# Stacking the high and low parts of the queries in the score products of a dilated-attention kernel

## The chip, the cores and the metric

The kernel runs on one core of one Trainium2 chip. The metric is the device time of one execution in microseconds (us). The engines of the core go by these names: PE is TensorE (matmuls; PEld is its weight loads), DVE is VectorE, ACT is ScalarE, POOL is GpSimd, and SP issues most of the DMAs.

## What is computed

Two layers over 1024 positions of width 1024, batch 1, all in float32. Layer 0 mixes tokens with a chunked gating MLP, layer 1 with dilated sliding-window attention. A dense MLP with squared ReLU follows each mixer. The diff touches the attention of layer 1 alone, of which this is the core (cut from the reference):

```python
WINDOW_DILATIONS = ((128, 1), (512, 4), (2048, 16))     # 3 groups, 8 heads of 64 in each
def _dilated_group(q, k, v, bias_table, window, dilation):
    ...
    s = jnp.einsum('bnqrhc,bnkrhc->bnrhqk', qb, kc) * (HEAD_DIM ** -0.5)
    ...
    logits = jnp.where(valid[None, :, None, None], s + bias[None, None, None], NEG_INF)
    m = jnp.max(logits, axis=-1)
    p = jnp.exp(logits - m[..., None])
    den = jnp.sum(p, axis=-1)
    num = jnp.einsum('bnrhqk,bnkrhc->bnqrhc', p, vc)
    ...
```

The three groups are merged for each head by their denominators, and a projection follows.

## The kernel before

**Precision.** Products run in the float32r format. A float32 operand is split into a high part (a rounding copy on ACT) and a low part (source minus high part, on DVE). A product is then the sum of three: high by high, high by low, low by high.

**Units of attention.** Two heads of 64 channels lie together on the 128 partitions. There are 4 such head pairs and 3 dilation groups, so 12 units, taken for each pair in the order group 1, group 2, group 0 (dilations 4, 16, 1). `unit_qk` computes q and k of a unit (128 channels by 1024 positions) with seven block products instead of eight, in a Strassen-like scheme, each of 12 matmuls of 512 columns. Their results come up one half of the positions at a time, and `halves` (lines 1432 to 1437) makes the high and low parts of such a half: one ACT activation and one DVE operation over 128 partitions by 512 columns. It is called four times in a unit: q first half, k second half, q second half, k first half. The results go to four tiles of 128 by 1024, in an order of positions that puts the positions of one residue side by side. So for the dilations 4 and 16 the write has a stride (`permuted`, line 1216), and for dilation 1 it is contiguous.

**Scores.** `scores` (line 1491) is called four times in a unit (48 times in all), each time for two blocks of 128 queries and two heads. Each block and head takes three products of 64 rows (the channels of one head); head 0 lies on rows 0 to 63, head 1 on rows 64 to 127, and the products of the two heads alternate. The moving operand has 128 or 256 columns of keys. That is 12 products in a call. Behind it, DVE adds the bias and takes the extreme (line 1511), ACT takes the exponential (line 1513), PE transposes the probabilities (line 204), ACT and DVE split them (lines 225 and 226), and PE multiplies by the values; ACT and DVE then take that result out (lines 1551 and 1552).

**Order.** The order of PE's instructions is the order in which the program writes them. A small planner (`Flow`) advances a clock with each matmul (columns times 0.422 ns) and slips the steps of scores, transposes and value products between the block products when their due time on that clock has come; the scores of a unit are due 4200 ns of that clock after its q and k were issued. `flow.until` holds the second k half of a unit back until the scores of the unit before were issued. The order on the other engines is the scheduler's; operations marked `high_priority` are taken as if they stood 60 instructions earlier.

**Memory.** A pool `tpool` holds 13 temporaries of 128 by 512 under the tag "t" and 4 landing buffers under the tag "r" (`raw`, line 178), into which weights are loaded. PSUM's eight banks are three for block products ("mm") and five for the rest ("at").

Of the kernel before, what the change touches and what calls it, by code (L numbers as in the profile page):

```python
# [12 lines left out]
F32 = mybir.dt.float32  # L13
F32R = mybir.dt.float32r
AF = mybir.ActivationFunctionType
ALU = mybir.AluOpType
# [3 lines left out]
P = 128  # L20
D = 1024
S = 1024
HALF = 512
# [12 lines left out]
def blk(b, n=1):  # L36
    return slice(b * P, (b + n) * P)
# [91 lines left out]
def trunk(ctx: ExitStack, tc: tile.TileContext, xT, w_u, w_v, w_o, w_s, b_s, w_qkv, w_vt, w_bo, rel,  # L129
          w_up, w_dn, w_dl, vecs, onehot, outT):  # L130
    nc = tc.nc
# [5 lines left out]
    tpool = ctx.enter_context(tc.tile_pool(name="tpool", bufs=13))  # L137
# [2 lines left out]
    psa = ctx.enter_context(tc.tile_pool(name="psa", bufs=8 - MMB, space=PSUM))  # L140
    dram = ctx.enter_context(tc.tile_pool(name="dram", bufs=2, space=DRAM))
    ctx.enter_context(tc.manual_schedule(engines={mybir.EngineType.PE}))

    def temp():
        return tpool.tile([P, HALF], F32, tag="t", name="t")
# [7 lines left out]
    def slot(shape=(P, S), dtype=F32, name="s"):  # L153

        return slots.tile(list(shape), dtype, tag="s", name=name)
# [20 lines left out]
        return Pair(wpool.tile([P, 2, HALF], F32R, tag="w", name=name))  # L176

    def raw():
        return tpool.tile([P, HALF], F32, tag="r", name="r", bufs=4)

    def load(src, t=None):

# [7 lines left out]
    def mm_bank():  # L190
        return psm.tile([P, HALF], F32, tag="mm", name="mm")
# [4 lines left out]
    def matmul(out, lhsT, rhs, passes=1, **kw):  # L196
        nc.tensor.matmul(out, lhsT, rhs, **kw)  # L197
        n = 1
        for d in rhs.shape[1:]:
            n *= d  # L200
        flow.pe(max(n, 64) * COL * passes)
# [154 lines left out]
    def product(bank, w, xs, more=False):  # L356

        for k, x in enumerate(xs):
            three(bank, w, blk(k), x, not more and k == 0, k == len(xs) - 1, skip_group_check=True)
            flow.pump()  # L360
# [373 lines left out]
    for gi, chunks in enumerate(((0, 1, 2), (3, 4, 5), (6, 7))):  # L734
        banks = {}
        for k in range(KT):
# [35 lines left out]
            for e, i, n, f in order:  # L772
                x, c = ys[n // 4][k], blk(n % 4)
                matmul(banks[n, f], x[e == 1][:, c], w[e == 2][:, half(f)], start=(k == 0 and e == 0),
                       stop=(k == 7 and e == 2))
# [29 lines left out]
    for tiles in ((0, 1, 2), (3,), (4,), (5, 6, 7)):  # L805
# [3 lines left out]
        for s in range(2):  # L809
            for i, m in enumerate(tiles):  # L810
                b = mm_bank()
# [9 lines left out]
    for tiles in ((0, 1), (2,), (3,), (4, 5, 6, 7)):  # L821
        w = [weight(w_o[m]) for m in tiles]
        for s in range(2):
            for i, m in enumerate(tiles):
                b = mm_bank()
# [356 lines left out]
    hd = [[dram.tile([P, HALF], F32, name=f"hd{m}_{s}", bufs=1) for s in range(2)] for m in range(KT)]  # L1182
# [10 lines left out]
    def bias_tile(hp, g):  # L1193

        off = bvec.offset + (2 * hp * 3 + g) * VEC
        rev = temp()
        w = 2 * P if g < 2 else P
        if g < 2:
            nc.sync.dma_start(rev.rearrange("p (a b) -> p a b", a=2),
                              bass.AP(tensor=bvec.tensor, offset=off, ap=[[1, P], [3 * VEC, 2], [1, 2 * P]]))  # L1200
        else:
            nc.vector.memset(rev[:, 0:2 * P], NEG)
            for r in range(2):
                nc.sync.dma_start(
                    rev[64 * r:64 * r + 64, 0:2 * P].rearrange("p (a b) -> p a b", a=2)[:, :, 64 - 64 * r:128 - 64 * r],
                    bass.AP(tensor=bvec.tensor, offset=off + 64, ap=[[1, 64], [3 * VEC, 2], [1, 64]]))
        return rev, w

    def bias_turn(rev, w):
        t = spare().rearrange("p (a b) -> p a b", a=2)  # L1210
        src = rev[:, 0:2 * w]
        nc.vector.tensor_copy(t[:, :, 0:w], bass.AP(tensor=src.tensor, offset=src.offset + w - 1,
                                                    ap=[list(src.ap[0]), [w, 2], [-1, w]]))
        return t

    def permuted(t, s, g):

        d = DIL[g]
        if g == 0:
            return t[:, half(s)]  # L1220
        n = HALF // d
        return t.rearrange("p (r q) -> p q r", r=d)[:, s * n:(s + 1) * n, :]

    def own(t, g):
        return t if g == 0 else t.rearrange("p (q r) -> p q r", r=DIL[g])
# [8 lines left out]
    for hp, g in units:  # L1234
        u = Unit()
# [154 lines left out]
    def v_load(i):  # L1390

        u = U[i]
        if 0 < i < NU - 1:
            yield U[i - 1].pv, 0
        u.V = [slot((P, 4, 4, 64), F32R, "V") for _ in range(2)]
        src = vd[i // 4][:, i % 4]
        for e in range(2):
            t = u.V[e].bitcast(F32).rearrange("p b a c -> p b (a c)")
            if u.g == 0:
                parts = [(t, src.rearrange("(e b p) a c -> e p b (a c)", e=2, p=P)[e])]  # L1400
            elif u.g == 1:
                parts = [(t, src.rearrange("(e p b) a c -> e p b (a c)", e=2, p=P)[e])]
            else:
                x = src.rearrange("(q e b r) a c -> e r q b (a c)", q=64, e=2, b=4)
                parts = [(t[64 * r:64 * r + 64], x[e, r]) for r in range(2)]
            for dst, part in parts:
                vloads[i] = nc.sync.dma_start(dst, part).ins
        yield LAT["vd"]
        u.v.t = flow.t
# [5 lines left out]
    def unit_qk(i):  # L1415

        u = U[i]
        g, w = u.g, unit_w[i]
        if i == 0:
            u.bias = bias_turn(*u.rev)  # L1420
        if i < NU - 1:
            flow.add(v_load(i))
            U[i + 1].rev = bias_tile(U[i + 1].hp, U[i + 1].g)
        x = terms_a.t
        qk = {}

        def place_of(m, s):
            if m not in qk:
                qk[m] = [slot((P, S), F32R, f"{'qk'[m]}{e}") for e in range(2)]
            return [permuted(t, s, g) for t in qk[m]]  # L1430

        def halves(m, s, src):
            hi, lo = place_of(m, s)
            sc = -0.125 if m == 0 else 1.0
            with tc.high_priority(offset=PRIO):
                nc.scalar.activation(hi, src, AF.Copy, scale=sc)
                nc.vector.scalar_tensor_tensor(lo, src, sc, hi.bitcast(F32), op0=ALU.mult, op1=ALU.subtract)

        def total(x0, x1, t=None):
            t = temp() if t is None else t  # L1440
            with tc.high_priority(offset=PRIO):
                nc.vector.tensor_tensor(t, x0, x1, op=ALU.add)
            return t

        def copied(out, src):
            with tc.high_priority(offset=PRIO):
                nc.scalar.activation(out, src, AF.Copy)
            return out

        a = mm_bank()  # L1450
        product(a, w[1], x[1])
        more()
        sums = copied(mm_bank(), a)
        d = mm_bank()
        product(d, w[5], x[5])
        more()
        k1 = copied(temp(), d)
        product(sums, w[6], x[6], True)
        more()
        q1 = copied(temp(), sums)  # L1460
        product(a, w[2], x[2], True)
        more()
        halves(0, 0, own(a, g))
        product(sums, w[7], x[7], True)
        more()
        if i > 0:
            flow.until(lambda: U[i - 1].scored.t is not None)
        if i < NU - 1:
            U[i + 1].bias = bias_turn(*U[i + 1].rev)
        halves(1, 1, own(total(k1, sums, k1), g))  # L1470
        product(d, w[3], x[3], True)
        more()
        halves(0, 1, own(total(q1, d, q1), g))
        product(sums, w[4], x[4], True)
        more()
        halves(1, 0, own(sums, g))
        u.q, u.k = qk[0], qk[1]
        u.qk.t = flow.t

# [11 lines left out]
    def scores(u, j):  # L1491
        keys, at, width = geometry(u.g, j)
        sb = [at_bank(), at_bank()]
        for i in range(2):
            kc = blk(*keys[i])
            c = slice(at[i], at[i] + keys[i][1] * P)
            for a, b in ((0, 0), (0, 1), (1, 0)):
                for hd in range(2):
                    r = slice(64 * hd, 64 * hd + 64)
                    matmul(sb[hd][:, c], u.q[a][r, blk(2 * j + i)], u.k[b][r, kc],  # L1500
                           start=(a == 0 and b == 0), stop=(a == 1))
        ps = []
        for hd in range(2):
            p = temp()
            for i in range(2):
                w = keys[i][1] * P
                c = slice(at[i], at[i] + w)
                m, dn = u.st[:, 2 * j + i, hd, 0:1], u.st[:, 2 * j + i, hd, 1:2]
                bt = u.bias[:, hd, 0:P] if u.g == 2 else u.bias[:, hd, 2 * P - w:2 * P]
                with tc.high_priority(offset=PRIO):  # L1510
                    nc.vector.tensor_tensor_reduce(out=p[:, c], in0=sb[hd][:, c], in1=bt, op0=ALU.add, op1=ALU.min,
                                                   scale=1.0, scalar=BIG, accum_out=m)
                    nc.scalar.activation(p[:, c], p[:, c], AF.Exp, bias=m, scale=-1.0, accum_out=dn)
            ps.append(p)
        return ps
# [297 lines left out]
    for i in range(NU):  # L1813
        unit_qk(i)
# [136 lines left out]
```

## Time and profile before

| | |
|---|---|
| median of 3 runs | 2115.53 us (2114.2 to 2117.39) |
| the profiled execution, its own time | 2117.96 us |
| its span, first to last instruction | 2116.2 us, mean granted TensorE clock 0.998 |
| busy over the span | PE 99%, PEld 82%, DVE 75%, ACT 56%, POOL 23% |
| score products | 576, from 1073.2 to 1428.5 us of the span |

Times in the profile count from the span's start. A group of instructions has its line in the kernel, its engine, the output and input tiles by name, the shape, a count, the busy time in us and the mean of one in ns, and behind the bar the idle time just ahead of them with what ended it. L197 and L204 are the lines of the helpers for all matmuls and all transposes. Matmuls overlap in the pipeline, so the pace of PE is read from the starts and not from the durations.

### The profile page before, as it was taken

The numbers are of one execution on the slowest core, as the hardware profiler recorded it, in microseconds if no ns is written. First come the engines' busy times: TensorE is split into PE (matmuls) and PEld (weight loads), VectorE is DVE, ScalarE is ACT, GpSimd is POOL, SyncE is SP. The second block draws the span as 40 slices with busy tenths as digits, with TensorE's granted clock in tenths as the row PEclk, the third lists the DMA queues.
The fourth block names the chain that finished last, engine by engine and source line by source line (L and its number), as shares of the span: only waits on it lengthen the run. The fifth ranks groups of instructions, "written<-read, shape, count | busy, mean of one in ns | idle before, by whom it ended". The sixth has DMA issues, their size and how long they took to land.

```text
span 2116.2 us, 30735 instructions
## 1 busy us (share of the span) xinstructions
PE 2093.6 (99%) x10160; PEld 1731.2 (82%) x10160; DVE 1577.5 (75%) x2902; ACT 1182.7 (56%) x2387; POOL 495.5 (23%) x368
## 2 busy tenths in 40 slices
PE   9999999999999999999999999999999999999998
PEld 7888888888888888788888888888888888888887
DVE  7878769766689999787746666757985456988876
ACT  7645436566675555345456665776556556544432
POOL 2000124323224333430000000002442222433244
PEclk9999999999999999999999999999999999999999
DMA  6428814588766666644865657582266443655432
GB/s 220 130 94 294 305 34 139 196 281 278 258 208 204 231 209 225 222 162 164 308 194 160 176 156 185 157 270 79 71 205 198 156 154 127 203 164 161 143 115 80
DMA packets 224757, 387.10 MB, mean 183 GB/s; under 512 B 39898, under 2 KB 67669, under 8 KB 224597
## 3 DMA queue, kind: packets, MB, share of 16 engines
q1 hardware_dynamic: 215456, 383.77, 55.1%
q10 hardware_dynamic: 9140, 1.36, 0.4%
q8 instruction: 80, 1.31, 0.3%
q14 instruction: 81, 0.66, 0.1%
HBM read 252.24 MB, written 132.81 MB: 182 GB/s over the span
## 4 chain that ended last, share of the span: by engine, by line
PE 88%; DVE 6%; DMA 3%; issue 1%; ACT 1%; POOL 0%; SPq 0%; DVEq 0%; POOLq 0%; ACTq 0%
PE mm L197 45%; PE at L197 41%; PE at L204 2%; DVE y L226 1%; DMA t<-in_w_qkv 1%; DVE t L226 1%; DMA r<-in_w_v 1%; DMA h<-in_xT 0%; DVE r L443 0%; DVE hx L226 0%; DVE tr L226 0%; DVE wp L226 0%; DMA t<-hid_(1, 0)_6229 0%; DMA r<-in_w_vt 0%; DVE b L448 0%
## 5 line engine op out<-in xcount | busy, mean ns | idle before, releaser
L226 DVE TENSOR_TENSOR wp<-r,wp 128x512 fp32r<-128x512 f32 (+3 forms) x399 | 328.2, 828 | 121.8 <-ACT wp L225 119.2
L225 ACT ACTIVATE wp<-r 128x512 fp32r<-128x512 f32 (+3 forms) x399 | 236.0, 596 | 316.7 <-PE at L197 194.5
L197 PE MATMUL mm<-t,wp 128*128 128x512 f32 x1368 | 345.2, 396 | 0.2 <-DVE t L1001 0.2
L197 PE MATMUL at<-hx,wp 128*128 128x512 f32 x1452 | 341.1, 389 | 1.7 <-DVE h L1079 1.5
L197 PEld LDWEIGHTS at<-hx,wp 128*128 128x128 f32 x1452 | 272.2, 188 | 60.0 <-DVE h L1079 3.2
L197 PEld LDWEIGHTS mm<-t,wp 128*128 128x128 f32 x1368 | 250.7, 188 | 53.0 <-issue 0.7
L283 POOL TENSOR_TENSOR t<-t 128x512 f32<-128x512 f32 (+1 forms) x60 | 76.2, 1271 | 810.3 <-ACT t L278 808.1
L197 PE MATMUL at<-y,wp 128*128 128x512 f32 x1008 | 245.3, 389 | 0.0
L197 PE MATMUL mm<-hx,wp 128*128 128x512 f32 x984 | 234.3, 389 | 0.1
L197 PEld LDWEIGHTS at<-y,wp 128*128 128x128 f32 x1008 | 189.1, 188 | 39.5 <-issue 0.4
L197 PEld LDWEIGHTS mm<-hx,wp 128*128 128x128 f32 x984 | 184.6, 188 | 38.9 <-ACT mm L1102 0.5
L197 PE MATMUL mm<-y,wp 128*128 128x512 f32 x816 | 210.3, 397 | 1.2 <-DVE y L226 0.6
L381 POOL TENSOR_TENSOR t<-r 128x512 f32<-128x512 f32 (+3 forms) x62 | 82.5, 1331 | 477.7 <-DMA r<-in_w_up 121.3
L197 PEld LDWEIGHTS mm<-y,wp 128*128 128x128 f32 x816 | 149.1, 188 | 33.4 <-DVE y L226 1.1
L226 DVE TENSOR_TENSOR hx<-t,hx 128x512 fp32r<-128x512 f32 x192 | 161.5, 845 | 6.5 <-ACT hx L225 6.3
L197 PE MATMUL mm<-y,whi 128*128 128x512 f32 x512 | 158.4, 390 | 1.2 <-DVE t L789 1.2
L197 PE MATMUL at<-t,wp 128*128 128x512 f32 x552 | 130.6, 389 | 0.0
L225 ACT ACTIVATE hx<-t 128x512 fp32r<-128x512 f32 x192 | 118.7, 627 | 20.8 <-DMA t<-hid 12.5
L383 POOL TENSOR_TENSOR r<-r 128x512 f32<-128x512 f32 (+3 forms) x62 | 91.0, 1468 | 167.2 <-DVE wp L226 146.9
L197 PEld LDWEIGHTS at<-t,wp 128*128 128x128 f32 x552 | 103.6, 188 | 21.5
L1079 DVE TENSOR_TENSOR h<-h,at 128x512 f32<-128x512 f32 x144 | 97.6, 678 | 25.6 <-PE at L197 25.1
L197 PEld LDWEIGHTS mm<-y,whi 128*128 128x128 f32 x512 | 95.5, 188 | 21.0 <-issue 1.6
(247 smaller groups left out, 3481.3 us busy)
## 6 DMA issues: line engine op xcount, KB each, us to landing
t<-hid SPq DMA_DIRECT2D x182, 256.0 KB, 4.2
wd<-tr SPq DMA_DIRECT2D x154, 256.0 KB, 3.1
wp<-wd SPq DMA_DIRECT2D x77, 512.0 KB, 4.2
hid<-t SPq DMA_DIRECT2D x140, 256.0 KB, 2.9
r<-in_w_up SPq DMA_DIRECT2D x120, 256.0 KB, 2.9
r<-in_w_dn SPq DMA_DIRECT2D x80, 256.0 KB, 2.6
hid<-b SPq DMA_DIRECT2D x56, 256.0 KB, 2.9
r<-in_w_v SPq DMA_DIRECT2D x48, 256.0 KB, 3.1
```

What stands on the lines that cost most here:

```text
L197: nc.tensor.matmul(out, lhsT, rhs, **kw)
L204: nc.tensor.transpose(out, src, ident)
L225: return (nc.scalar.activation(hi, src, AF.Copy).ins, (engine or nc.vector).tensor_tensor(lo, src, hi.bitcast(F32), op=ALU.subtract).ins)
L226: (engine or nc.vector).tensor_tensor(lo, src, hi.bitcast(F32), op=ALU.subtract).ins)
L283: nc.gpsimd.tensor_tensor(self.acc, self.acc, sq, op=ALU.add)
L381: tt(r3, r[0, 0], r[1, 0], op=ALU.subtract)
L383: tt(r[1, 1], r[1, 0], r[0, 0], op=ALU.subtract)
L1079: return engine.tensor_tensor(hs[i, s], hs[i, s], src, op=ALU.add).ins
```

## The change

The query tiles and the key tiles are laid out anew, by head. For head 0 the query tile has the high part on rows 0 to 63 and the low part on rows 64 to 127; for head 1 it is the other way round. The key tile of a head has the high part of that head's keys on both halves of the rows. A third tile has the low parts of the keys of both heads. One product over 128 rows of a head's query tile and key tile then gives high by high and low by high at once, and one product over 64 rows with the third tile gives high by low. A call of `scores` has 4 products of 128 rows and then 4 of 64 rows.

`halves` is cut by head: two ACT activations and two DVE operations over 64 partitions each, and for k two more ACT copies, which are not marked `high_priority`, to fill the other half of the rows. The source of the last `halves` of a unit is first copied from PSUM to a temporary by ACT. The third tile has two buffers of 128 by 1024, for which room is made by closing the pool of the four landing buffers `raw`; the helper `roomy` opens one of the two pools at a time in the same place.

```diff
+    def roomy(name, bufs):
+        if name not in held:
+            room.close()
+            held.clear()
+            held[name] = room.enter_context(tc.tile_pool(name=f"{name}{len(opened)}", bufs=bufs))
+            opened.append(name)
+        return held[name]
...
     def raw():
-        return tpool.tile([P, HALF], F32, tag="r", name="r", bufs=4)
+        return roomy("raws", 4).tile([P, HALF], F32, tag="r", name="r")
+
+    def lows():
+        return roomy("lows", 2).tile([P, S], F32R, tag="kl", name="kl")
...
-                qk[m] = [slot((P, S), F32R, f"{'qk'[m]}{e}") for e in range(2)]
+                qk[m] = [slot((P, S), F32R, f"{'qk'[m]}{e}") for e in range(2)] + [lows()] * m
             return [permuted(t, s, g) for t in qk[m]]
 
         def halves(m, s, src):
-            hi, lo = place_of(m, s)
+            to = place_of(m, s)
             sc = -0.125 if m == 0 else 1.0
+            rows = [slice(0, 64), slice(64, 128)]
             with tc.high_priority(offset=PRIO):
-                nc.scalar.activation(hi, src, AF.Copy, scale=sc)
-                nc.vector.scalar_tensor_tensor(lo, src, sc, hi.bitcast(F32), op0=ALU.mult, op1=ALU.subtract)
+                for hd, r in enumerate(rows):
+                    nc.scalar.activation(to[hd][r], src[r], AF.Copy, scale=sc)
+                for hd, r in enumerate(rows):
+                    lo = to[2][r] if m else to[hd][rows[1 - hd]]
+                    nc.vector.scalar_tensor_tensor(lo, src[r], sc, to[hd][r].bitcast(F32), op0=ALU.mult,
+                                                   op1=ALU.subtract)
+            if m:
+                for hd, r in enumerate(rows):
+                    nc.scalar.activation(to[hd][rows[1 - hd]], to[hd][r].bitcast(F32), AF.Copy)
...
-        halves(1, 0, own(sums, g))
+        halves(1, 0, own(copied(temp(), sums), g))
...
-            for a, b in ((0, 0), (0, 1), (1, 0)):
-                for hd in range(2):
-                    r = slice(64 * hd, 64 * hd + 64)
-                    matmul(sb[hd][:, c], u.q[a][r, blk(2 * j + i)], u.k[b][r, kc],
-                           start=(a == 0 and b == 0), stop=(a == 1))
+            for hd in range(2):
+                matmul(sb[hd][:, c], u.q[hd][:, blk(2 * j + i)], u.k[hd][:, kc], start=(i == 0), stop=False,
+                       skip_group_check=True)
+        for i in range(2):
+            kc = blk(*keys[i])
+            c = slice(at[i], at[i] + keys[i][1] * P)
+            for hd in range(2):
+                r = slice(64 * hd, 64 * hd + 64)
+                matmul(sb[hd][:, c], u.q[hd][r, blk(2 * j + i)], u.k[2][r, kc], start=False, stop=(i == 1),
+                       skip_group_check=True)
```

More of the change, by code (lines that the diff above doesn't have):

```diff
@@ L142, in trunk @@
     ctx.enter_context(tc.manual_schedule(engines={mybir.EngineType.PE}))
+    room = ExitStack()
+    ctx.enter_context(room)
+    held = {}
+    def roomy(name, bufs):
[5 more added lines that the diff above has]
+        return held[name]
+    opened = []
     def temp():
```

## The prediction

> **What bounds the kernel now.** I read the page first, then the busy time by stretch over the attention stage, then the timeline around a few score blocks.
>
> ```profile
> span 2116.2 us, 30735 instructions
> PE 2093.6 (99%) x10160; PEld 1731.2 (82%) x10160; DVE 1577.5 (75%) x2902; ACT 1182.7 (56%) x2387; POOL 495.5 (23%) x368
> ...
> PE 88%; DVE 6%; DMA 3%; issue 1%; ACT 1%; POOL 0%; SPq 0%; DVEq 0%; POOLq 0%; ACTq 0%
> ```
>
> PE is busy 99% of the span and carries 88% of the chain that ended last. So the time falls only where PE gets less to do, and rises by every stall that the change puts into PE's order. The diff acts in the twelve attention units, about 1058 to 1418 us, plus four score blocks just after.
>
> ```profile
> core 0: us, PE busy (x) PEld busy (x) DVE busy (x) ACT busy (x) POOL busy (x), PEclk, DMA share, GB/s
> 1058.00:1418.00 360.00, 358.06 (x2242) 295.15 (x2241) 228.53 (x737) 231.12 (x652) 0.00 (x0) 1.00 0.62 186
> ```
>
> PE has 2 us of idle in 360; ACT works 64% and DVE 63% of the stage, at full clock. That looks like room for more work on ACT and DVE, but it is a mean, and below I look at the stretches where the new work would lie.
>
> **What the score products cost today.** 576 products of 64 rows, twelve to a block, 48 blocks. The next fence holds the two groups, then weight loads seen through two slits of 10 to 15 ns, then PE around two score blocks and one value block.
>
> ```profile
> L197 PE MATMUL at<-k,q 64*128 64x128 f32 x312 | 26.2, 285 | 1.9 <-DVE t L1688 1.9
> L197 PE MATMUL at<-k,q 64*128 64x256 f32 x264 | 23.3, 294 | 0.0
> 1073.33 0.19 PEld L197 LDWEIGHTS at<-k,q 64*128 64x128 f32 x2
> 1073.44 0.19 PEld L197 LDWEIGHTS at<-k,q 64*128 64x128 f32 x2
> 1073.23 0.96 PE L197 MATMUL at<-k,q 64*128 64x128 f32 x12
> 1074.12 0.97 PE L197 MATMUL mm<-t,wp 128*128 128x512 f32 x3
> ...
> 1085.37 1.03 PE L197 MATMUL at<-tr,V 128*128 128x256 f32 x8
> 1086.24 0.90 PE L197 MATMUL mm<-t,wp 128*128 128x512 f32 x3
> 1086.98 0.82 PE L204 MATMUL at<-ident,t 128*128 128x128 f32 x6
> 1087.73 0.95 PE L197 MATMUL at<-k,q 64*128 64x128 f32 x12
> ```
>
> The weight loads of the two heads (rows 0 to 63 and 64 to 127) run together: both slits show two loads of 0.19 us begun in the same hundredth, the next two 0.11 later. So twelve products are six slots of two. A block takes 1074.12 - 1073.23 = 0.89 us: six slots of 0.11 = 0.66, and 0.23 for starting and for going back to 128 rows. The value block, eight products of 128 rows, takes 1086.24 - 1085.37 = 0.87, or 0.109 each, and those go one by one.
>
> **PE's part of the change.** Removed: six double slots, 0.66. Added: four products of 128 rows, 4 x 0.109 = 0.44, and two double slots, 0.22. Together 0.66 again. A product over 128 rows costs as much as two over 64 that run side by side, so stacking high and low saves a product, not a slot. The 0.23 stays, because there is still one passage from 128 to 64 rows and one back. I take 0. Six transposes take 1087.73 - 1086.98 = 0.75 before a score block instead of 6 x 0.109 = 0.65, so a passage is worth about 0.10: if it hides better, or costs once more, that is 0.10 x 48 = 5 us down or up. [...]
>
> **ACT and DVE, the operations.** Times in ns are least, median and greatest of twelve; the least is a unit of dilation 1 (written contiguously, 4 units), the median one of dilation 4 or 16 (written with a stride, 8 units).
>
> ```profile
> L1436 ACT ACTIVATE q<-mm x12: 570/1082/1093, 1060.5 to 1397.7; 128x512 fp32r<-128x512 f32 x12
> L1436 ACT ACTIVATE q<-t x12: 631/1124/1135, 1066.8 to 1407.4; 128x512 fp32r<-128x512 f32 x12
> L1437 DVE SCALAR_TENSOR_TENSOR q<-t,q x12: 691/1096/1205, 1067.9 to 1408.0; 128x512 fp32r<-128x512 f32 x12
> L1447 ACT ACTIVATE t<-mm 128x512 f32<-128x512 f32 x24 | 14.1, 587 | 5.5 <-PE mm L197 5.1
> L1551 ACT ACTIVATE N<-at 64x256 f32<-64x256 f32 x96 | 36.4, 379 | 35.0 <-DVE N L1552 20.1 <-PE at L197 11.1 <-PE at L204 2.1
> L225 ACT ACTIVATE tr<-at 128x256 fp32r<-128x256 f32 x32 | 10.5, 377 | 8.6 <-PE at L204 8.5
> L1552 DVE TENSOR_TENSOR N<-N,at 64x256 f32<-64x256 f32 x96 | 40.1, 417 | 52.8 <-ACT N L1551 52.0
> L226 DVE TENSOR_TENSOR tr<-at,tr 128x256 fp32r<-128x256 f32 x32 | 12.2, 419 | 9.8 <-ACT tr L225 9.6
> ```
>
> An activation over 64 partitions takes what one over 128 takes (379 against 377 ns for 256 elements), and so on DVE (417 against 419). So each of the four `halves` of a unit, now cut by head, costs twice its ACT and twice its DVE time; each of the two for k adds two ACT copies; and one ACT copy of PSUM to a temporary (0.59) comes in. The moves between partition halves are nothing new: line 1551 does them.
>
> In a strided unit ACT gains one activation for each q half (1.08 + 1.12), three for each k half (6 x about 1.1) and 0.59: 9.4 us. Neighbours overlap by about 0.1 us in the timeline, which leaves about 8.6. In a contiguous unit it is 8 x 0.6 + 0.59 = 5.4, with overlap 5.0. DVE gains four operations: 4 x 1.1 = 4.4 or 4 x 0.69 = 2.8. Over twelve units that is 8 x 8.6 + 4 x 5.0 = 89 us on ACT, 231 + 89 = 320 of 360: no bound yet by the mean.
>
> The copies read and write with a stride; no ACT row has both. DVE's low part reads the strided high part and writes with a stride, at 1.10 against 0.69 contiguous, no worse than ACT's strided write alone (1.12 against 0.63). So I take 1.1; if reading cost a second 0.49, it would be 32 copies x 0.49 = 16 us of ACT more, and a gain is excluded, since a copy is not shorter than the contiguous 0.6. [...]
>
> **Where they lie.** Scores of a unit begin when its q and k are there, and PE's order is fixed. I take for each kind of unit the stretch from its first write of q to its first score product: there all the added work must be done. The last four rows below show how that is read for the fifth unit (group 2).
>
> ```profile
> 1060.40:1073.20 12.80, 12.80 (x57) 10.33 (x56) 5.63 (x6) 6.30 (x6) 0.00 (x0) 1.00 0.73 250
> 1083.50:1102.30 18.80, 18.80 (x113) 15.72 (x111) 13.68 (x35) 12.49 (x33) 0.00 (x0) 1.00 0.69 178
> 1142.40:1162.60 20.20, 20.18 (x130) 16.89 (x126) 17.47 (x60) 15.64 (x38) 0.00 (x0) 1.00 0.46 145
> 1177.40:1196.50 19.10, 18.46 (x113) 15.26 (x112) 15.88 (x33) 13.22 (x28) 0.00 (x0) 1.00 0.53 167
> 1209.00:1225.50 16.50, 16.50 (x99) 13.68 (x97) 9.03 (x26) 8.10 (x24) 0.00 (x0) 1.00 0.61 169
> 1177.44 1.08 ACT L1436 ACTIVATE q<-mm 128x512 fp32r<-128x512 f32 x1 [0.37 <-DVE t L1688]
> ...
> 1192.17 1.07 ACT L1436 ACTIVATE k<-mm 128x512 fp32r<-128x512 f32 x1
> ...
> 1193.63 1.14 DVE L1437 SCALAR_TENSOR_TENSOR k<-mm,k 128x512 fp32r<-128x512 f32 x1
> ...
> 1196.46 0.89 PE L197 MATMUL at<-k,q 64*128 64x128 f32 x12
> ```
>
> ACT's busy time is the fourth figure with a count. First unit: 6.3 + 8.6 - 12.8 = 2.1 us too much. Second: 12.5 + 8.6 - 18.8 = 2.3. Fourth (group 1, later parts; the seventh and tenth are built alike): 15.6 + 8.6 - 20.2 = 4.0, three times. Fifth (with the eighth and eleventh): 13.2 + 8.6 - 19.1 = 2.7, three times. The contiguous units: 8.1 + 5.0 is under 16.5, nothing. Sum: 2.1 + 2.3 + 12.0 + 8.1 = 24.5 us by which PE stands before a unit's first scores. DVE in the fourth: 17.5 + 4.4 = 21.9 in 20.2, over by less than ACT, so it is not added.
>
> The chain of one unit says the same. In the fifth, k is ready at 1193.63 + 1.14 = 1194.77, 1.69 us ahead of the scores. Behind the last product there would now be a copy (0.59), two activations (2.2) and two copies (2.2) instead of 1.07 + 1.14 on ACT and DVE: 5.0 against 2.2 is 2.8 longer, 1.1 over the slack, with the doubled q part queued ahead of it. In ACT's queue the next unit's copies, exponentials and value evacuations stand behind these, and PE's transposes and value products wait on those.
>
> Two corrections, one each way: splits for value products that are due only after the scores can wait (about 1 us in each of eight stretches, 8 less); and idle time of ACT between dependent steps does not vanish (about 1 each, 8 more). I take them as equal. The staging copy frees its PSUM bank one step earlier; no row shows a wait there, so 0. The kernel's planner counts a third fewer score columns (a third of the groups' 26.2 + 23.3 = 49.5 us), so its steps shift by a little over a microsecond in a unit; the PE wait in the first group's row, 1.9 us over three blocks, is the size of such an effect: I take 0, with 6 either way as the bound over twelve units. The pool swap happens twice (raws to lows, and back after the last unit); the raw loads of both sides are far from it: 0, at most a microsecond each.
>
> **Sum.** The profiled execution took 2117.96 us, 1.7 outside its span and 2.4 above the median of 2115.53. 2118 + 0 (PE) + 24 = 2142 on its scale, and 2139.5 against the median. Own range: 8 less for deferred work and 5 for PE; 8 more for idle, 5 for PE, 6 for the order and 2 for the pools: 2126 to 2161.
>
> **Rivals.** (1) The new work is hidden: other ACT work in the stretch, about 11 of the 15.6 us in the fourth unit, slides past the scores without PE missing it. It decides once 4 us of those can slide. For it: ACT's 36% idle. Against: what slides are exponentials and splits that PE reads within a few microseconds. PE then moves by 0 to -5: 2110.5 to 2115.5, say 2113. Chance 0.15, part of it within 0.2% (about 4 us, what a measurement of this kernel can tell from no change). (2) The products really go down by a third: 49.5 / 3 = 16.5 us less, 2099. It needs slots that hold one product, and the two slits show two; also ACT hidden. 0.04. (3) Worse: strided copies at 1.6 us add 16 us of ACT in the eight tight stretches, or, not being marked urgent, wait behind other ACT work: 2139.5 + 16 = 2155.5, up to 2170. Against: the DVE row above. 0.15. [...] (4) Forecast: 0.66.
>
> **Numbers.** Faster by over 0.2%: 0.04 + 0.08 = 0.12; within: 0.07 of rival 1; slower: 0.66 + 0.15 = 0.81. The range 2117 to 2168 leaves out most of rivals 1 and 2 and the far end of 3, about 0.2.
>
> **What would show it.** Score blocks with 8 products, still about 0.89 us long; activations over 64 partitions at 0.6 or 1.1 us; ACT near 90% in the stage; PE's weight load of the first score product idle 2 to 4 us behind an ACT copy of k in eight of twelve units. It is wrong if blocks shrink to 0.6 us, if those stalls are missing, or if the time goes to value products or to a stage after 1428 us.

## The result and the profile after

| | before | changed |
|---|---|---|
| median of 6 runs each | 2117.56 us (2114.2 to 2119.81) | 2185.19 us (2182.59 to 2189.61) |
| ratio, with its 95% interval | | 1.0322 (1.0308 to 1.0337) |
| the profiled execution, its span | 2116.2 us | 2185.6 us |
| mean granted TensorE clock | 0.998 | 0.987 |

The change costs 67.6 us, 3.2%. Slower was forecast, by 24 us, with 2168 us as the upper end. The time lies above it.

The page of the changed kernel: the span, the busy time by engine, the granted clock in 40 slices, and the chain that ended last.

```profile
span 2185.6 us, 30503 instructions
PE 2120.4 (97%) x9968; PEld 1754.1 (80%) x9968; DVE 1623.7 (74%) x2950; ACT 1281.0 (59%) x2495; POOL 496.4 (23%) x368
...
PEclk9999999999999999999899999999999999999999
...
PE 39%; ACT 5%; DVE 5%; issue 1%; DMA 1%; POOL 0%; SPq 0%; ACTq 0%; DVEq 0%; POOLq 0%
```

ACT has 98 us more (1281.0 against 1182.7), where the working had 89, and DVE 46 more, as the working had it. PE fell from 99% to 97% of the span and from 88% to 39% of the chain, and one of the 40 slices has less than 90% of full clock (the 8). Where PE waited in the attention stage of the changed kernel (what it waited for, total us, times, longest):

```profile
PE at L213 <- DVE tr L242: 15.0, 9, 3.5
PE at L213 <- ACT tr L241: 6.2, 3, 2.1
PE mm L213 <- ACT t L1471: 5.3, 2, 3.5
PE at L220 <- ACT t L1695: 4.8, 3, 1.6
PE at L213 <- DVE t L1717: 3.6, 3, 1.2
PE at L213 <- ACT k L1461: 2.5, 4, 0.8
PE at L220 <- DVE N L1581: 2.3, 3, 0.8
PE mm L213 <- ACT mm L1811: 1.8, 1, 1.8
PE at L213 <- DVE st L1540: 1.0, 4, 0.3
```

These nine rows sum to 42.5 us. In the same stretch (1058 to 1488 us) the kernel before has 2.8 us of such waits. Only 2.5 us of the 42.5 are at the k copies ahead of a unit's first scores. Half of it, 21.2 us, is at `tr`: the split probabilities, which the value products read. One such wait, in the unit whose stretch the prediction showed: ACT, then DVE, then PE of the changed kernel, in order of time.

```profile
1217.76 2.45 ACT L1454 ACTIVATE q<-t 64x512 fp32r<-64x512 f32 x2 [1.09 <-DVE t L1466]
1219.97 0.45 ACT L1580 ACTIVATE N<-at 64x256 f32<-64x256 f32 x1
1220.44 0.49 ACT L241 ACTIVATE tr<-at 128x384 fp32r<-128x384 f32 x1
...
1218.93 1.23 DVE L1457 SCALAR_TENSOR_TENSOR q<-t,q 64x512 fp32r<-64x512 f32 x1 [0.28 <-ACT q L1454]
1220.45 0.42 DVE L1581 TENSOR_TENSOR N<-N,at 64x256 f32<-64x256 f32 x1 [0.29 <-ACT N L1580]
1220.89 1.04 DVE L1457 SCALAR_TENSOR_TENSOR q<-t,q 64x512 fp32r<-64x512 f32 x1
1221.96 1.02 DVE L242 TENSOR_TENSOR tr<-at,tr 128x384 fp32r<-128x384 f32 x2
...
1218.89 0.28 PE L213 MATMUL at<-tr,V 128*128 128x256 f32 x1
1222.57 1.02 PE L213 MATMUL at<-tr,V 128*128 128x256 f32 x7 [3.40 <-DVE tr L242]
```

In the kernel before, the same value block ran through:

```profile
1190.30 1.13 ACT L1436 ACTIVATE q<-t 128x512 fp32r<-128x512 f32 x1
...
1191.46 1.21 DVE L1437 SCALAR_TENSOR_TENSOR q<-t,q 128x512 fp32r<-128x512 f32 x1 [0.34 <-ACT q L1436]
...
1192.46 1.29 PE L197 MATMUL at<-tr,V 128*128 128x256 f32 x8
```

The changed kernel's PE begins it at 1218.89 and stands 3.40 us at its second product. The split it needs is on ACT behind two urgent activations for q (2.45 us where one took 1.13), and on DVE behind two operations for q (2.27 us where one took 1.21). The work that was added for q stands ahead of work that PE reads sooner.

The stalls have a second price. The first of them is a block product that waits until ACT has copied a PSUM bank out:

```profile
1072.97 3.43 PE L213 MATMUL mm<-t,wp 128*128 128x512 f32 x9 [1.83 <-ACT t L1471]
```

Around and after it (clock is the figure behind POOL's count):

```profile
1071.00:1073.00 2.00, 0.17 (x2) 0.03 (x1) 1.72 (x2) 1.92 (x4) 0.00 (x0) 1.00 0.95 281
...
1074.00:1076.00 2.00, 2.00 (x6) 1.34 (x4) 1.81 (x2) 1.95 (x3) 0.00 (x0) 0.50 0.05 18
...
1084.00:1086.00 2.00, 2.00 (x6) 1.52 (x6) 0.89 (x6) 1.86 (x8) 0.00 (x0) 0.50 0.01 4
```

PE worked for 0.17 of two microseconds, and from 1074 to beyond 1086 the granted clock is half (0.50). In that time six block products take 2.93 us, where the kernel before needs 1.65 for six of the same kind (the changed kernel, then the one before):

```profile
1079.15 2.93 PE L213 MATMUL mm<-t,wp 128*128 128x512 f32 x6
```

```profile
1103.09 1.65 PE L197 MATMUL mm<-t,wp 128*128 128x512 f32 x6
```

Over the whole span the clock withheld is 2185.6 x (1 - 0.987) = 28 us, against 2116.2 x (1 - 0.998) = 4 before. So up to 24 us of the loss is half clock, and at least 44 is something else; the waits above account for 40 of it (42.5 less the 2.8 of before). The 24 is an upper bound, since PE was not always able to use the clock. PE's busy time suggests that most of it counts: it is 2120.4 us here, 2093.6 in the kernel before, and 2091.4 in `e2c_products_charged` below, which has the same number of products as the changed kernel and, like the kernel before, a mean clock of 0.998. Here the half clock came within a microsecond of a wait of 1.83 us, which ended at 1072.97.

The score block itself is what the prediction made of it: four products over 128 rows, then four of 64.

```profile
1196.38 0.62 PE L213 MATMUL at<-k,q 128*128 128x128 f32 x4
1196.93 0.49 PE L213 MATMUL at<-kl,q 64*128 64x128 f32 x4
1197.36 1.20 PE L213 MATMUL mm<-t,wp 128*128 128x512 f32 x4
```

It runs from 1196.38 to 1197.36, 0.98 us, against 0.89 before. The difference is about the 0.10 us that the prediction took for the passage to 64 rows: it lay ahead of the block and lies inside it now. From the start of the last block product to the start of the score block, the kernel before takes 0.33 us (1196.13 to 1196.46) and the changed one 0.23 (1196.15 to 1196.38).

### The profile page after: what moved, and what is told of

Read it like the earlier page. It is cut to its first block, busy times and chain, and to the rows that moved or that the text cites. A ratio compares the mean times of both kernels' runs of the same rounds, so it can differ in the third digit from the quotient of the medians.

```text
span 2185.6 us, 30503 instructions
## 1 busy us (share of the span) xinstructions
PE 2120.4 (97%) x9968; PEld 1754.1 (80%) x9968; DVE 1623.7 (74%) x2950; ACT 1281.0 (59%) x2495; POOL 496.4 (23%) x368
## 4 chain that ended last, share of the span: by engine, by line
PE 39%; ACT 5%; DVE 5%; issue 1%; DMA 1%; POOL 0%; SPq 0%; ACTq 0%; DVEq 0%; POOLq 0%
PE mm L213 20%; PE at L213 18%; ACT k L1454 1%; ACT q L1454 1%; ACT k L1461 1%; PE at L220 1%; DVE kl L1457 1%; ACT t L1542 1%; DMA ex<-sc 0%; DVE tr L242 0%; DVE q L1457 0%; ACT tr L241 0%; DVE t L1466 0%; ACT N L1580 0%; DVE t L1717 0%
## 5 line engine op out<-in xcount | busy, mean ns | idle before, releaser
L213 PE MATMUL mm<-t,wp 128*128 128x512 f32 x1368 | 358.6, 405 | 5.5 <-ACT t L1471 5.3
L213 PEld LDWEIGHTS mm<-t,wp 128*128 128x128 f32 x1368 | 257.3, 194 | 60.6 <-ACT t L1471 6.4
L213 PE MATMUL mm<-y,wp 128*128 128x512 f32 x816 | 205.6, 395 | 1.1 <-DVE y L242 0.6
```

## The experiments

Differences below are against the runs of the kernel before that share the chip with them. "Clock at most" is worked out as above from span and mean clock.

**The products alone, and the planner's count.** The scores are written as in the change; the halves stay as before, so the stacked layout is left out and the scores are other numbers.

```diff
# e2_products_only
-            for a, b in ((0, 0), (0, 1), (1, 0)):
...
+                matmul(sb[hd][:, c], u.q[hd][:, blk(2 * j + i)], u.k[hd][:, kc], start=(i == 0), stop=False, ...)
...
+                matmul(sb[hd][:, c], u.q[hd][r, blk(2 * j + i)], u.k[1][r, kc], start=False, stop=(i == 1), ...)
# e2c_products_charged: and behind the second matmul, for each head
+                flow.pe(keys[i][1] * P * COL)
```

> The score blocks have four products of 128 rows and four of 64 as in the changed kernel, but the halves are as before, one ACT and one DVE operation over 128 partitions. This leaves out the stacked layout: the 128 rows hold both heads, so the scores are other numbers. Load theory: within 5 us of the kernel before, 2112 to 2121 us, with blocks of about 0.8 to 0.9 us. Rival, products or planner make the loss: 2140 us or more. Rival, PE really saves a third: 2100 us.

> e2_products_only (which leaves out the stacked layout), but the planner is charged for twelve products in each block as before, so that the order of PE comes back to that of the kernel before. Planner theory: the 12 us of e2_products_only come from steps packed closer at a unit's end, and go: within 4 us of before or a little under. Rival, the 128-row products themselves cost: still 2126 to 2132.

Measured: 2129.65 us, 12 over before (ratio 1.006, 1.0045 to 1.0075), and with the planner charged as before 2116.74, ratio 0.9999 (0.9989 to 1.0009). So four products of 128 rows and four of 64 cost what twelve of 64 cost, and the first 12 us come from PE's order alone. In `e2_products_only` PE waits at the merge of a head pair's three groups, where steps were packed closer:

```profile
PE at L204 <- ACT t L1671: 4.8, 3, 1.6
PE at L197 <- DVE t L1693: 3.7, 3, 1.2
```

`e2c_products_charged` also shows what stacked tiles would give if they cost ACT and DVE nothing: no gain, with PE's order as it was. Other orders were not tried with it.

**All the ACT and DVE work, old products.** The halves are cut by head and staged, the k copies are made and read, but in the old layout.

```diff
# e1_work_only, against the changed kernel
-                    nc.scalar.activation(to[hd][r], src[r], AF.Copy, scale=sc)
+                    nc.scalar.activation(to[0][r], src[r], AF.Copy, scale=sc)
...
-                    nc.scalar.activation(to[hd][rows[1 - hd]], to[hd][r].bitcast(F32), AF.Copy)
+                    nc.scalar.activation(to[2][r], to[0][r].bitcast(F32), AF.Copy)
...
+            for a, b in ((0, 0), (0, 1), (1, 2)):
```

> All the new ACT and DVE work and the third key tile, but the score blocks keep their twelve products of 64 rows (low by high reads the copied key tile, so PE waits for the copies as in the changed kernel), and the planner counts as before. Load theory (ACT's and DVE's added operations make the loss, PE's products are worth nothing): as slow as the changed kernel, 2175 to 2195 us. Rival, the products of 128 rows or the planner's smaller count make the loss: 2115 to 2145 us.

Measured: 2174.52 us, 57.0 over before (ratio 1.027, 1.0254 to 1.0285). Most of the loss is this work, with half clock at most 24 us in it (mean clock 0.987). That is a hair under the 2175 that the load theory asked for, and far from the rival's 2145. The remaining 10.6 us to the changed kernel would fit the 12 of `e2`, but `e6_after_charged` below gives the order only about 4 of them. About 7 are left to the new layout itself.

**The work piece by piece.** The kernel before, with its halves cut by head on both engines, with and without the staging copy, and on each engine alone; and the staging copy alone.

```diff
# e9_staging_only, and in all of e5, e5a, e5d
-        halves(1, 0, own(sums, g))
+        halves(1, 0, own(copied(temp(), sums), g))
# ACT cut: e4, e5, e5a
-                nc.scalar.activation(hi, src, AF.Copy, scale=sc)
+                for r in (slice(0, 64), slice(64, 128)):
+                    nc.scalar.activation(hi[r], src[r], AF.Copy, scale=sc)
# DVE cut: e4, e5, e5d
-                nc.vector.scalar_tensor_tensor(lo, src, sc, hi.bitcast(F32), op0=ALU.mult, op1=ALU.subtract)
+                for r in (slice(0, 64), slice(64, 128)):
+                    nc.vector.scalar_tensor_tensor(lo[r], src[r], sc, hi[r].bitcast(F32), op0=ALU.mult, ...)
```

> The kernel before with each half cut by head: two ACT and two DVE operations over 64 partitions for one of each; no copies, no staging, old layout, old products. It adds about 45 us to ACT and 45 us to DVE. Load theory with a limit that is reached step by step: 20 to 35 us over before, 2136 to 2152. Rival, the loss comes from the k copies and the longer chain of a unit alone: within 5 us of before.

> e4_cut_by_head with the staging copy of the last k half added (one ACT copy more in a unit). In e4_cut_by_head PE waited up to 4.4 us for a bank of block products, which the four cut operations hold longer than the two before. Bank theory: the staging copy frees the bank, about 15 to 19 us come back, 2160 to 2168 us. Rival, those waits are ACT's load: not better than e4, 2180 or more.

> The kernel before with the staging copy and the halves cut by head on ACT alone (two activations over 64 partitions, one DVE operation over 128). ACT gains about 52 us, DVE nothing. ACT as the limit: nearly all of e5's loss, 2150 or more. DVE as the limit, or the two in turn: 2125 to 2140.

> The kernel before with the staging copy and the halves cut by head on DVE alone. DVE gains 45 us, ACT only the 7 us of staging. ACT as the limit: within 8 us of before. DVE as the limit: nearly all of e5's loss, 2150 or more. Both in turn: 2125 to 2140.

> The kernel before with the staging copy alone, 12 ACT copies of 0.59 us in all. It is the common base of e5, e5a and e5d. If staging is free: within 3 us of before. If it costs by lengthening the way to a unit's first scores by 0.6 us: 2119 to 2124.

| | time (us) | over before | mean clock | clock at most |
|---|---|---|---|---|
| e9_staging_only | 2118.95 | 2.2 | 0.998 | 0 |
| e5a_act_cut_staged | 2135.83 | 19.2 | 0.998 | 0 |
| e5d_dve_cut_staged | 2148.90 | 32.3 | 0.993 | 11 |
| e5_cut_staged | 2155.98 | 39.4 | 0.992 | 13 |
| e4_cut_by_head | 2181.71 | 64.2 | 0.987 | 24 |
| e1_work_only | 2174.52 | 57.0 | 0.987 | 24 |
| changed kernel | 2185.19 | 67.6 | 0.987 | 24 |

The times are medians, the clock is that of the profiled execution. For `e5a_act_cut_staged` that one took 2130.67 us; its three others took 2135.42 to 2137.44 us at a mean clock of 0.994, which is about 9 us of clock at most.

Three readings. First, `e4_cut_by_head`, with neither the k copies nor the staging copy, was nearly as slow as the whole change; my 20 to 35 us were far off. The staging copy, which adds work, takes 25 us off it. The bank theory is that without it the four cut operations hold the PSUM bank of the last product, and the next product waits for that bank. The profile of `e4_cut_by_head` names no releaser for those waits (18.7 us, five of them). The one in the second fence ends 0.10 us behind DVE operations that read k from such a bank: they end at 1223.09, and PE begins at 1223.19.

```profile
PE mm L197 <- issue: 18.7, 5, 5.0
```

```profile
1220.97 2.12 DVE L1439 SCALAR_TENSOR_TENSOR k<-mm,k 64x512 fp32r<-64x512 f32 x2 [0.97 <-ACT k L1437]
...
1223.19 1.19 PE L197 MATMUL mm<-t,wp 128*128 128x512 f32 x2 [4.26 <-issue]
```

The row falls out in `e5_cut_staged`, as the bank theory wants, and the time falls by more than its 15 to 19 us; up to 11 of the 25 us is clock (24 against 13). Second, DVE alone costs more than ACT alone, though I had left DVE out of the sum. If all of the half clock counts, DVE alone costs about 21 us without it, and ACT alone 14, by its profiled execution at 0.998. DVE alone had a mean clock of 0.990 to 0.993 in all four runs, ACT alone 0.994 in three and 0.998 in one. Third, from `e5` to `e1` the k copies (and the third tile) cost 18 us, of which up to 11 is clock.

**The copies on an idle engine.**

```diff
# e3_copies_on_pool, against the changed kernel
-                    nc.scalar.activation(to[hd][rows[1 - hd]], to[hd][r].bitcast(F32), AF.Copy)
+                    nc.gpsimd.tensor_copy(to[hd][rows[1 - hd]], to[hd][r].bitcast(F32))
```

> The changed kernel with the k copies on POOL, which has no work in this stage. ACT is freed of 46 us. Load theory with ACT as the limit: 25 to 40 us under the changed kernel, 2145 to 2160. Rival, DVE or the length of the chain is the limit: within 10 us of the changed kernel, or slower if POOL's copy takes over 2 us.

Measured: 2177.2 us, 59.7 over before; 8 us under the changed kernel where the load theory had 25 to 40. Freeing ACT of 44 us (1281.0 to 1237.0) does little. Of the 21.2 us of waits at `tr`, 17.6 stay, and PE now also waits 4.5 us for POOL's copies:

```profile
PE at L213 <- DVE tr L242: 14.1, 10, 3.0
PE at L213 <- POOL k L1461: 4.5, 4, 1.3
```

So "ACT is the limit" is wrong; ACT's copies are only a part.

**Queue or path.** One operation of the added kind is put beside the chain: it is urgent, as long as the others, and nothing reads its result.

```diff
# e10_dve_beside (against e9, with the third tile): behind each low part
+                nc.vector.scalar_tensor_tensor(more_, src[r], sc, hi[r].bitcast(F32), op0=ALU.mult, op1=ALU.subtract)
# e11_act_beside: behind each high part
+                nc.scalar.activation(more_, src[r], AF.Copy, scale=sc)
```

> e9 (before with staging) with one DVE operation more behind each low part, over 64 partitions, urgent, into a third tile that nothing reads. DVE has the same added time as in e5d_dve_cut_staged (32 us over before), but q and k are ready as early as before. Queue theory (the operations behind it on DVE, splits and softmax, come late): 15 to 32 us over before, 2132 to 2149. Path theory (only the longer way to q and k counts): within 5 us of before.

> The same on ACT: one activation more behind each high part, over 64 partitions, urgent, into a third tile that nothing reads; the added time is that of e5a_act_cut_staged (19 us over before). Queue theory: 10 to 19 us over before, 2127 to 2136. Path theory: within 5 us of before.

Measured: 2143.18 us on DVE, 26.1 over before (ratio 1.0123, 1.0108 to 1.0139), and 2121.88 on ACT, 4.8 over (1.0023, 1.0013 to 1.0034). DVE is busy 39 us more than in `e9`, and ACT in the other run 43. On DVE the queue makes most of the loss (26 of the 32 of `e5d_dve_cut_staged`, with half clock at most 9 and 11 in them, at mean clocks of 0.994 and 0.993): what stands behind the new operations is late, whether their result is wanted or not. The new operation also reads its source, so it could hold a PSUM bank longer; but no block product waits for one in `e10_dve_beside` (its one `mm` row, 0.9 us, is there before too). In the next fence DVE of `e10_dve_beside` runs the wanted and the unwanted operation, then the split; PE stands 0.70 us at its transposes, until that split is done.

```profile
1187.62 1.11 DVE L1458 SCALAR_TENSOR_TENSOR q<-mm,q 128x512 fp32r<-128x512 f32 x1
1188.63 1.05 DVE L1459 SCALAR_TENSOR_TENSOR kl<-mm,q 64x512 fp32r<-64x512 f32 x1
1189.60 1.00 DVE L242 TENSOR_TENSOR tr<-at,tr 128x384 fp32r<-128x384 f32 x2
...
1190.20 1.05 PE L220 MATMUL at<-ident,t 128*128 128x128 f32 x4 [0.70 <-DVE tr L242]
```

On ACT it is the other way round: queue time costs 5, and cutting the activation costs 19. With the cut, DVE's low parts also wait for the second half of the high part. DVE's idle time for q and k, in `e5a_act_cut_staged` and then in the kernel before:

```profile
DVE q L1438 <- ACT q L1437: 36.7, 18, 10.1
DVE k L1438 <- ACT k L1437: 19.0, 15, 2.4
```

```profile
DVE q L1437 <- ACT q L1436: 25.0, 18, 7.1
DVE k L1437 <- ACT k L1436: 2.4, 3, 1.2
```

Of the 28 us more, 4 come with the staging copy: `e9` alone has 24.2 and 7.1. In `e11_act_beside` the like waits of DVE sum to 37.2, only 6 over `e9`, and that run cost 4.8. How the other 24 reach PE is not settled. PE's waits in `e5a_act_cut_staged` are 4.3 us at a unit's keys and 2.4 at the splits, so part is the longer way to the scores, and part the splits that stand behind in DVE's queue.

**PE's order and the due times.**

```diff
# e6_after_charged: the changed kernel, the planner charged for twelve products (as e2c)
# e7_after_later / e13_after_earlier: the changed kernel, LAT
-soft=5500.0, turn=4200.0, ... qk=4200.0
+soft=7000.0, turn=7000.0, ... qk=7500.0      # e7
+soft=4000.0, turn=3000.0, ... qk=4200.0      # e13
# e12_scores_due_early: the kernel before
-qk=4200.0
+qk=1400.0
# e8_after_plain_halves: the changed kernel, halves outside high_priority
```

> The changed kernel with the planner charged for twelve products in each block, as before. In e2 and e2c that charge was worth 13 us. Additive theory: the same here, 2170 to 2176 us. Rival, with ACT and DVE late anyway the order matters less: within 5 us of the changed kernel, 2180 to 2190.

> The changed kernel with later due times in the planner: scores 7500 instead of 4200 ns after q and k, transposes 7000 instead of 5500 after scores, value products 7000 instead of 4200 after transposes. Lateness theory (PE meets splits and keys that are merely late): PE has other products in between, 2140 to 2165. Rival, ACT and DVE cannot keep up in the stage, or the steps then crowd at a unit's end: no better than the changed kernel, 2180 or more.

> The changed kernel with earlier due times: transposes 4000 instead of 5500 ns after scores, value products 3000 instead of 4200 after transposes. Later times cost 61 us in e7. If the crowding at a unit's end is a large part of the loss, earlier times give some back: 2165 to 2180. If PE then only meets unfinished splits more often: 2190 or more.

> The kernel before with the scores due 1400 instead of 4200 ns after q and k were issued: no work is added, but PE comes to a unit's first scores 2.8 us sooner, as if the way to k were 2.8 us longer. Path theory by the slacks of 1.7 to 4.3 us: PE waits about 1.1 us in three units and 0.4 in four, 5 us, 2119 to 2126. Rival, such a wait upsets the steps behind it as well: 2130 or more; or PE gains by looser unit ends: 2115 or less.

> The changed kernel with the halves not marked urgent, so that softmax and splits are no longer queued behind them. Queue theory (PE stands at value products because the splits are behind the halves on ACT and DVE): those stalls fall, those of the first scores grow, the sum 2160 to 2180. Rival, the amount of work decides and not its place: within 5 us of 2185, or slower where the scores come late.

Measured: e6 2180.9 us, 64.1 over before, about 4 under the changed kernel, against 12 where nothing else was late; with intervals of 1.0281 to 1.0325 and 1.0308 to 1.0337 that may be nothing. But the order moves the place of the waits: the two merge rows of `e2` (4.8 and 3.6 in the changed kernel) come down to 2.5 in e6, the waits for the splits to 16.3, and those at the k copies rise from 2.5 to 10.4, in four of the twelve units.

```profile
PE at L213 <- ACT k L1461: 10.4, 8, 1.7
```

The others: e7 2246.26, e13 2202.69, e8 2195.25: all slower than the changed kernel. e12 2154.94, 38 over before without any added work. My theory of mere lateness falls with e7: with later due times PE waits longest for the copy behind a unit's first block product and for value loads, as if it had nothing left to put in between.

```profile
PE mm L213 <- ACT mm L1471: 26.3, 7, 5.1
PE at L213 <- DMA V<-vd: 16.7, 7, 4.2
```

And e12 does not test the path by itself, as I had meant: the shorter lead moved the steps behind as well, and its largest wait is at the merge, 9.9 us, ahead of 8.7 at k (ACT's high parts, below, and 3.5 for DVE's low parts). The 8.7 is still more than the 5 that the path theory gave. All waits of its profiled execution sum to 18.6 us, and half clock is at most 24 in it (mean clock 0.987; 0.989 to 0.991 in the three others).

```profile
PE at L204 <- ACT t L1666: 9.9, 3, 3.3
PE at L197 <- ACT k L1436: 5.2, 3, 2.2
```

Putting the splits ahead of the halves (e8) only moved the wait. The waits for splits fall to 5.2 us, and its first scores now stand 18.3 us at the k copies:

```profile
PE at L213 <- ACT k L1461: 18.3, 14, 2.7
```

## Why the prediction was wrong

- **PE's part, taken as 0: right.** `e2c_products_charged` gives 0.9999. The slits that showed two loads at once decided it. The rival of a third less (2099) is out. The value block's 0.109 us a product was read too simply: its label names only the first form, and the block mixes four products of 256 columns with four of 128. In the trace the four of 128 begin 0.059 or 0.114 us ahead of the next product, 0.087 on average. At that pace, four products in 48 blocks would be an estimated 4 us less than by the row; that did not come (`e2c_products_charged`, 0.9989 to 1.0009, or about 2 us either way).
- **The operations: right.** Activations over 64 partitions took 1.08 to 1.11 us in a strided unit, the copies 1.10 and not 1.6, so rival 3's stride was not it. ACT was busy 330 of the 430 us of the stage, 77%, and not near 90%.

```profile
L1454 ACT ACTIVATE q<-t x24: 626/1108/1350, 1070.1 to 1473.6; 64x512 fp32r<-64x512 f32 x24
L1461 ACT ACTIVATE k<-k x48: 627/1104/1186, 1067.7 to 1479.5; 64x512 fp32r<-64x512 f32 x48
```

- **Where they lie: the step that failed.** I added up ACT's busy time to a unit's first scores, called DVE "over by less than ACT, so it is not added", and placed all stalls at those scores. DVE's cut alone costs 32 us and ACT's 19. PE's waits are at the splits for the value products (21.2 of 42.5 us) and hardly at the k copies (2.5). A correction of 8 us for splits that "can wait" had the wrong sign: they are what PE reads next. The prediction's own sign of being wrong, time that goes to value products, is what came. I had also counted the idle time of both engines as room for more work, with 8 us against it on ACT. On DVE it was not room: 39 us more of work whose result nothing reads cost 26 (`e10_dve_beside`). On ACT it nearly was: 43 cost 4.8. How much stands at the k copies depends on PE's order as well (10.4 us in e6).
- **The order, taken as 0 with 6 as bound: mis-sized.** It measured 12 us by itself (`e2` against `e2c`); in the changed kernel about 4 or nothing, since other waits took its place.
- **The clock: missing.** Up to 24 us. My row said full clock (1.00), and I carried that over to a kernel with stalls, which has 0.94 from 1058 to 1488 us.
- **The staging copy: small, as priced (2.2 us, with no change inside its interval of 0.9997 to 1.0016), its use missed.** No row of before showed a wait for that bank, because none occurred until the operations that read it were doubled.

In sum: of 67.6 us, about 39 come from cutting the halves by head (19 and 32 for each engine alone; they overlap), about 18 from the copies and the third tile, and about 11 from the rest: about 4 or nothing from the order, the rest, about 7 or more, from the new layout, whose cause is not shown. Up to 24 us of the whole is half clock. What stays open is how much of those 24 PE could have used, how the cut on ACT alone reaches PE, and why the same steps, packed a little differently, cost 38 us in `e12`; the runs show that the order is sensitive, not a rule for it. The cost of moving the low parts of q to the other partitions, by itself, was not tried; it lies within that rest.

## What to carry to other kernels

Before counting products saved, look whether the small ones already run in pairs: here two loads that began in the same hundredth of a microsecond meant that a stacked product replaced a pair, not two slots (ratio 0.9999). When work is added to an engine's queue beside a saturated PE, list what stands behind it in that queue and when PE reads that; the sum of busy time in a stretch does not tell (39 us more on DVE cost 26, 43 more on ACT cost 4.8). Beside short waits of PE there may be clock withheld, so a loss found by adding up waits can be too small (here 42.5 us of waits and up to 24 us of clock).

## What was not expected of the hardware

- PE waits of 1.8 to 3.5 us in the changed kernel were followed by half clock (0.50) for 3.4 to 14 us in several places of the attention stage (from 1074, 1111, 1180, 1224, 1289, 1333 and 1401 us). The length of one wait did not decide it: in `e10_dve_beside` two waits of 0.64 and 0.70 us within 3.2 us were followed by 3.4 us at about half pace (from 1190.20 us: four transposes in 0.70 us, where four at 1184.59 took 0.36, then six block products in 2.71), and in `e2_products_only` waits of up to 1.6 and 1.2 us were not followed by half clock (mean clock 0.998, as before). In the profiled execution of `e5a_act_cut_staged`, with no wait over 0.8 us, the clock stayed full (0.998); no row shows what its three runs at 0.994 waited for.
- A copy over 64 partitions with a stride on both sides took no longer on ACT (1.10 us) than one with a stride on the write alone (1.08 to 1.11), and POOL did the same copy in 1.13 us (medians; that of POOL over all 48 copies, 0.61 to 2.06).
